# Rounded weight parts by casting transfers instead of ScalarE in group two's input blocks, and a lane step tied to the split one k-step earlier

## The chip, the cores and the metric

The kernel runs on one core of one Trainium2 chip. The metric is the device time of one execution in microseconds; lower is better. Three runs of the kernel before gave 1782.76, 1782.76 and 1781.36 us, median 1782.76 us.

## What is computed

One layer of a bidirectional hybrid encoder is applied to two requests (1024 and 256 tokens, model width 2048):

```python
hn = rms_norm(x, norm_g)
proj = hn @ w_in                        # 2048 -> 4896
xbc, z_ssd, dt_raw, q, k, v, z_att, mq, z_mem = split_cols(proj, IN_SIZES)
o_ssd = rms_norm(ssd(silu(conv(xbc)), dt) * silu(z_ssd))
o_att = window_attention(rms_norm(q), rms_norm(k), v, sink) * silu(z_att)
mk, mv = split_cols(rms_norm(mem) @ w_mem_kv, ...)
o_mem = softmax(rms_norm(mq) @ rms_norm(mk).T) @ mv * silu(z_mem)
y = x + concat[o_ssd, o_att, o_mem] @ w_out
```

All arrays are float32. The large products are done with rounded parts: a float32 value is split into h, the value rounded to the type that TensorE multiplies quickly (float32r), and l, the rounded rest, and a product is the sum of h·h, h·l and l·h.

## The kernel before

**Groups and blocks.** The 1280 tokens make two groups of five 128-token tiles each. The program goes through them in blocks. Most of group one's input columns and the last half of group two's output are multiplied in pairs (`block_pair`, from line 1257); these and the memory's blocks are not touched by the change. Group two's input blocks come in this order: x0 to x5, kv, q, za0, za1, z0, z1, mq, zm0, zm1. Of these kv, q, z0, z1 and mq are built by `block_tok`, 16 k-steps each: a k-step takes one 128-row slice of the weights (512 columns, 288 for kv) and does three matmuls for each of five token tiles. The ten x, za and zm blocks are built by `block_feat`, 8 steps each of two slices of 256 columns, with 24 matmuls of 320 columns in a step. In both the last two steps are run together, tile by tile, so that the first accumulators are finished early. These 15 blocks have 160 weight loads. Then follow the four blocks o0 to o3 of the output, again by `block_tok`.

**A k-step's weights.** SyncE loads the slice into `wraw` (four buffers, `RB`). `wsplit` (line 204) makes the parts: ScalarE copies `wraw` to `wh` (line 206), VectorE subtracts `wh` from `wraw` to give `wl` (line 207). `wh` and `wl` have three buffers each (`WB`): the parts of step k can be written once the matmuls of step k-3 have run, while TensorE has the steps k-2 and k-1 in front of it.

**Lanes.** Beside the blocks runs all else: convolution, state-space scan, attention, normalisations. It is written as generators in two queues, `lanes`. After each k-step `pump` (line 158) takes some steps from them, at rates given by the table `RATES`. `step` (line 144) runs one of them:

```python
for ins in marks:
    st.enter_context(tc.issue_after(ins))
next(gen)
```

`issue_after` puts every instruction that the step issues on an engine behind `ins` on that engine's queue. `marks` holds the two instructions of the last `wsplit`: so a lane step's ScalarE work stands behind the last ScalarE split, and its VectorE work behind the last VectorE split. GpSimd does small things for the lanes: the power in a reciprocal root (lines 123 and 124), copies and clears of `lg`, `lgw` and `mprw` (lines 683 and 635); no mark names an instruction of GpSimd.

**Order on the engines.** Each engine runs its instructions in the order in which they stand. A scheduler sets that order from its own estimate of when operands are there; the splits are traced with a priority that is 100 places higher (`HP[2]`).

Of the kernel before, what the change touches and what calls it, by code (L numbers as in the profile page):

```python
# [10 lines left out]
F32 = mybir.dt.float32  # L11
# [10 lines left out]
KT = D // P  # L22
# [9 lines left out]
RATES = ({'kv': (4.0, 1.0), 'z1': (2.2, 1.7)},  # L32
         {'kv': (1.5, 1.5), 'x': (2.1, 2.15), 'q': (2.25, 2.5), 'za': (2.15, 2.5), 'z0': (2.1, 2.5),
          'z1': (2.1, 2.55), 'mq': (2.0, 2.7), 'zm': (1.75, 2.75), 'o': (2.15, 2.4)})
# [10 lines left out]
def hymba_encoder_kernel(  # L45
# [7 lines left out]
    V, A, G, T, S = nc.vector, nc.scalar, nc.gpsimd, nc.tensor, nc.sync  # L53
# [48 lines left out]
    def dram(shape, name):  # L102
        return dr.tile(shape, F32, tag=name, name=name)
# [5 lines left out]
    q_d = [dram([P, 512], f"q_{t}") for t in range(NT)]  # L109
# [28 lines left out]
    def queue(lane, fn, ts):  # L138
        for t in ts:
            lanes[lane].append(((fn.__name__, t), fn(t)))  # L140

    marks = []

    def step(lane):
        name, gen = lane[0]
# [32 lines left out]
    pend, loaded = deque(), deque()  # L178
# [25 lines left out]
    def wsplit(raw, h, l):  # L204

        a = A.activation(h, raw, AF.Copy)  # L206
        b = V.tensor_sub(l, raw, h.bitcast(F32))  # L207
        marks[:] = a.ins, b.ins

    def w_laid(src, n):  # L210

        def load(k, raw):
            S.dma_start(raw, src[k])
        return load, n

    def laid_in(name):
        o, n, tok_ = W_AT[name]
        flat = w_in_laid[o:o + D * n]
        return flat.rearrange("(k p c) -> k p c", p=P, c=n if tok_ else 512)

    def w_in_rows(name):
        return w_laid(laid_in(name), W_AT[name][1])
# [8 lines left out]
    TURNED = [4 * q + m for q in (0, 2, 1, 3) for m in range(4)]  # L231
    PAIRED = [k + 8 * i for k in range(8) for i in range(2)]

    def block_tok(w, nt, evac, before_last=None, feats=range(KT), places=range(KT)):

        load, n = w
        ps = [acc.tile([P, 512], F32, tag="acc", name="acc") for _ in range(nt)]
        hls = {}
        for k in range(KT):
            raw = wp.tile([P, 512], F32, tag="wraw", name="wraw", bufs=RB)  # L240
            load(feats[k], raw[:, :n])
            with tc.high_priority(offset=HP[2]):
                h = wp.tile([P, 512], F32R, tag="wh", name="wh", bufs=WB)
                l = wp.tile([P, 512], F32R, tag="wl", name="wl", bufs=WB)
                wsplit(raw[:, :n], h[:, :n], l[:, :n])
            hls[k] = h, l
            if k == KT - 2:
                continue
            if k == KT - 1 and before_last is not None:
                before_last(k)  # L250

            for t in range(nt):
                for k_ in ((k - 1, k) if k == KT - 1 else (k,)):
                    q, m = divmod(places[k_], 4)
                    h, l = hls[k_]
                    sh = cur["H", q][:, m, t * P:(t + 1) * P]
                    sl = cur["L", q][:, m, t * P:(t + 1) * P]
                    T.matmul(ps[t][:, :n], sh, h[:, :n], start=(k_ == 0), stop=False)  # L258
                    T.matmul(ps[t][:, :n], sh, l[:, :n], start=False, stop=False)  # L259
                    T.matmul(ps[t][:, :n], sl, h[:, :n], start=False, stop=(k_ == KT - 1))  # L260
                if k == KT - 1:
                    with tc.high_priority(offset=HP[0]):
                        evac(t, ps[t])
            if k == KT - 1:
                yield k - 1
            yield k

    def block_feat(name, evac):

        ps = [[acc.tile([P, 512], F32, tag="acc", name="acc") for _ in range(2)] for _ in range(2)]  # L270
        src = laid_in(name)
        hls = {}
        for kk in range(KT // 2):
            raw = wp.tile([P, 512], F32, tag="wraw", name="wraw", bufs=RB)
            S.dma_start(raw, src[kk])
            with tc.high_priority(offset=HP[2]):
                h = wp.tile([P, 2, 256], F32R, tag="wh", name="wh", bufs=WB)
                l = wp.tile([P, 2, 256], F32R, tag="wl", name="wl", bufs=WB)
                wsplit(raw, h.rearrange("p a c -> p (a c)"), l.rearrange("p a c -> p (a c)"))
            hls[kk] = h, l  # L280
            if kk == KT // 2 - 2:
                continue
            tail = kk == KT // 2 - 1

            for kks in ([(kk - 1, kk)] if tail else [(kk,)]):
                for f in range(2):
                    for k in [2 * x + j for x in kks for j in range(2)]:
                        q, m = divmod(k, 4)
                        sh, sl = [x[:, k % 2, f * P:(f + 1) * P] for x in hls[k // 2]]
                        for half in range(2):  # L290
                            c = slice(half * 320, half * 320 + 320)
                            o = ps[f][half][:, :320]
                            T.matmul(o, sh, cur["H", q][:, m, c], start=(k == 0), stop=False)  # L293
                            T.matmul(o, sh, cur["L", q][:, m, c], start=False, stop=False)  # L294
                            T.matmul(o, sl, cur["H", q][:, m, c], start=False, stop=(k == KT - 1))  # L295
                    if tail and f == 0:
                        with tc.high_priority(offset=HP[1]):
                            evac(0, ps[0])
            for k in range(2 * kks[0], 2 * kk + 2):
                yield k  # L300
        with tc.high_priority(offset=HP[1]):
            evac(1, ps[1])
# [20 lines left out]
    def ev_raw(dst, base):  # L323
        def f(i, ps):
            z = ev.tile([P, 512], F32, tag="evt" if i % 2 else "evu", name="qs")
            A.activation(z, ps, AF.Copy)
            S.dma_start(dst[base + i], z)
        return f

    def ev_dtkv(base):  # L330
        def f(i, ps):
            t = base + i
            r = ev.tile([P, P], F32, tag="evt" if i % 2 else "evu", name="kraw")
            A.activation(r, ps[:, 32:160], AF.Copy)
            S.dma_start(k_d[t], r)
            V.tensor_add(dt_all[:, t, :], ps[:, :32], dtb)
            V.tensor_copy(v_all[:, i + (2 if base else 0), :], ps[:, 160:288])  # L337
        return f


    left = deque()

    def some_left():
        with ExitStack() as st:
            for ins in marks:
                st.enter_context(tc.issue_after(ins))
            left.popleft()()
# [800 lines left out]
    raw, sums, rows = {}, {}, {}  # L1148
# [301 lines left out]
    def run(gen, rates, after=None, hold=0, lag=2, extra=None):  # L1450

        for k in gen:
            if after is not None:
                pend.extend(after(k))
            if hold:
                for _ in range(2 if k < KT - 4 else 0):
                    if pend:
                        u = pend.popleft()()
                        next(u)
                        next(u)  # L1460
            else:

                if loaded and (len(loaded) == lag or not pend or k >= KT - 4):
                    next(loaded.popleft())
                if pend and k < KT - 4:
                    loaded.append(pend.popleft()())
                    next(loaded[-1])

            if k >= hold:
                pump(rates)  # L1470
            if extra is not None:
                extra(k)
# [99 lines left out]
    run(block_tok(w_mem_rows(1), 4, ev_mv, places=TURNED), MR[1], extra=p_step)  # L1572

    def tok(name, w, evac, after=None, grp=0):
        run(block_tok(w, 5, evac), RATES[grp][name], after)

    def feat(name, b, evac, grp, after=None, extra=None):
        run(block_feat(f"{name}{b}", evac), [r / 2 for r in RATES[grp][name]], after, lag=3, extra=extra)
# [2 lines left out]
        extra=lambda k: p_step(16 + k))  # L1581
# [5 lines left out]
    for u, unit in enumerate(units):  # L1587
# [42 lines left out]
    w_kv = w_in_rows("kv")  # L1630
    run(block_tok(w_kv, 5, ev_dtkv(0), before_last=lambda _: need(vectors, [0])), RATES[0]["kv"], hold=5,
        extra=lambda k: some_left() if left else None)
# [4 lines left out]
    def when_done(n, then):  # L1637

        told = []

        def f(k):
            for _ in range(n):
                if left:
                    some_left()
            if not left and not told:
                told.append(then())
        return f
# [3 lines left out]
        extra=when_done(1, lambda: queue(1, ssd_up, range(4))))  # L1651
# [10 lines left out]

    need(attn, range(4))
    kv_shift()
    run(block_tok(w_kv, 5, ev_dtkv(5)), RATES[1]["kv"], extra=lambda k: some_left() if left else None)
    queue(0, k_prep, range(5, 10))
    queue(0, attn, [4])
    queue(1, dt_prep, [5])
    run(block_tok(w_in_rows("q"), 5, ev_raw(q_d, 5)), RATES[1]["q"], extra=when_done(2, lambda: queue(1, ssd_up, range(4, 8))))
    gate("za", 0)  # L1670
    queue(0, attn, range(5, 10))
    tok("z0", w_in_rows("z0"), ev_gate(0, 5), grp=1)
# [106 lines left out]
```

## Time and profile before

| | us |
|---|---|
| median of three runs | 1782.76 |
| the profiled execution, its own time | 1782.24 |
| its span, first to last instruction | 1780.5 |
| TensorE (PE) busy in the span | 1766.1 |
| VectorE (DVE) busy | 1245.5 |
| ScalarE (ACT) busy | 918.6 |
| GpSimd (POOL) busy | 550.2 |

In the rows of the profile a line such as `L207 DVE ... wl<-wraw,wh` names the code line, the engine, what is written and what is read; "idle before" is the time for which that engine stood still just before, with what ended it. A row of the windows view gives a stretch of the execution (us from the start) and each engine's busy time in it. The two lines of `wsplit` are one helper for all callers, so their groups mix all blocks unless a window or a tile is named. Group two's input blocks run from 589.6 us (x0) to 1318.6 us (end of zm1).

### The profile page before, as it was taken

To read this page: it belongs to the slowest core of one execution; us is meant where nothing else is said; L and a number is where in the kernel's file an instruction comes from. 1 tells how busy PE (TensorE), PEld (TensorE's weight loads), DVE (VectorE), ACT (ScalarE), POOL (GpSimd) and SP (SyncE) were. 2 spreads that over 40 slices of the span, in tenths; PEclk is the share of its full clock that TensorE was granted. 3 is DMA by queue.
4 is the path that set the end of the run, shared out by engine and by line. 5 is a ranking of instruction groups with operands and counts; after the bars stand their busy time and mean duration, and the time that the engine had idled before them with its cause. 6 is when DMAs were issued, how large, how long until landed. Compare 5 with 4: busy or idle time off the path is not lost.

```text
span 1780.5 us, 31950 instructions
## 1 busy us (share of the span) xinstructions
PE 1766.1 (99%) x11046; PEld 1611.0 (90%) x11046; DVE 1245.5 (70%) x2348; ACT 918.6 (52%) x2049; POOL 550.2 (31%) x960
## 2 busy tenths in 40 slices
PE   9999999999999999999999999999999999999999
PEld 7889999999998999999889988887988888889999
DVE  5596788888868877877765676557777654766665
ACT  5555455554434766656464566544446633543332
POOL 0105899998810110011000100011100000058775
PEclk9999999999999999999999999999999999999999
DMA  8553454445446644453635655557777854644442
GB/s 302 192 182 124 136 153 148 142 142 164 123 145 202 196 131 135 149 166 101 193 121 179 197 151 161 170 161 248 223 239 230 255 188 141 221 145 143 148 142 78
DMA packets 208211, 301.16 MB, mean 169 GB/s; under 512 B 19569, under 2 KB 86193, under 8 KB 208049
## 3 DMA queue, kind: packets, MB, share of 16 engines
q1 hardware_dynamic: 207904, 299.06, 53.6%
q8 instruction: 87, 1.43, 0.3%
q14 instruction: 76, 0.61, 0.1%
q10 hardware_dynamic: 144, 0.06, 0.0%
HBM read 236.36 MB, written 62.69 MB: 168 GB/s over the span
## 4 chain that ended last, share of the span: by engine, by line
PE 88%; DVE 5%; issue 3%; DMA 2%; ACT 1%; POOL 1%; SPq 0%; POOLq 0%; DVEq 0%; ACTq 0%
PE acc L258 11%; PE acc L260 10%; PE acc L259 10%; PE acc L1288 7%; PE acc L1286 7%; PE acc L1287 7%; PE acc L293 5%; PE acc L295 5%; PE acc L294 5%; PE accm L1287 3%; PE accm L1286 3%; PE accm L1288 3%; PE po L723 1%; PE py L988 1%; DVE wl L207 1%
## 5 line engine op out<-in xcount | busy, mean ns | idle before, releaser
L207 DVE TENSOR_TENSOR wl<-wraw,wh 128x512 fp32r<-128x512 f32 (+1 forms) x480 | 347.4, 725 | 229.9 <-ACT wh L206 224.3
L206 ACT ACTIVATE wh<-wraw 128x512 fp32r<-128x512 f32 (+1 forms) x480 | 292.1, 613 | 297.1 <-PE acc L260 150.5
L258 PE MATMUL acc<-wh,xH 128*128 128x512 f32 (+1 forms) x1088 | 418.7, 385 | 0.2 <-DVE v_all L337 0.2
L260 PE MATMUL acc<-wh,xL 128*128 128x512 f32 (+1 forms) x1088 | 410.1, 377 | 0.0
L259 PE MATMUL acc<-wl,xH 128*128 128x512 f32 (+1 forms) x1088 | 409.7, 377 | 0.0
L258 PEld LDWEIGHTS acc<-wh,xH 128*128 128x128 f32 x1088 | 204.5, 188 | 36.9 <-issue 2.9
L260 PEld LDWEIGHTS acc<-wh,xL 128*128 128x128 f32 x1088 | 204.2, 188 | 37.0 <-issue 0.2
L259 PEld LDWEIGHTS acc<-wl,xH 128*128 128x128 f32 x1088 | 204.6, 188 | 35.3 <-issue 1.2
L293 PE MATMUL acc<-xH,wh 128*128 128x320 f32 x640 | 202.5, 316 | 0.2 <-DVE zs L309 0.2
L294 PE MATMUL acc<-xL,wh 128*128 128x320 f32 x640 | 198.9, 311 | 0.0
L295 PE MATMUL acc<-xH,wl 128*128 128x320 f32 x640 | 198.2, 310 | 0.0
L206 ACT ACTIVATE sh<-ws 128x384 fp32r<-128x384 f32 x176 | 91.2, 523 | 207.1 <-POOL ws L1254 103.4
L207 DVE TENSOR_TENSOR sl<-ws,sh 128x384 fp32r<-128x384 f32 x176 | 124.2, 709 | 95.8 <-ACT sh L206 94.0
L1254 POOL TENSOR_TENSOR ws<-wraw 128x128 f32<-128x128 f32 x176 | 111.1, 631 | 208.8 <-DMA wraw<-in_w_in_pairs_dram 93.6
L293 PEld LDWEIGHTS acc<-xH,wh 128*128 128x128 f32 x640 | 120.1, 188 | 2.7 <-issue 1.9
L294 PEld LDWEIGHTS acc<-xL,wh 128*128 128x128 f32 x640 | 120.2, 188 | 1.7 <-issue 1.4
L1254 POOL TENSOR_TENSOR ws<-wraw,ws 128x128 f32<-128x128 f32 x176 | 117.5, 667 | 13.8
L295 PEld LDWEIGHTS acc<-xH,wl 128*128 128x128 f32 x640 | 120.2, 188 | 0.7 <-issue 0.6
L1254 POOL TENSOR_TENSOR wraw<-wraw 128x128 f32<-128x128 f32 x176 | 112.6, 640 | 13.7
L1254 POOL TENSOR_TENSOR ws<-ws,wraw 128x128 f32<-128x128 f32 x176 | 116.2, 660 | 0.0
L635 POOL MEMSET lgw<- 128x1 f32 x40 | 3.9, 98 | 315.9 <-DVE lg L698 227.0
L362 DVE SCALAR_TENSOR_TENSOR c<-u,vec,c 128x638 f32<-128x638 f32 (+1 forms) x96 | 90.0, 939 | 9.1 <-ACT c L357 8.7
(439 smaller groups left out, 3951.0 us busy)
## 6 DMA issues: line engine op xcount, KB each, us to landing
wraw<-in_w_in_laid_dram SPq DMA_DIRECT2D x176, 256.0 KB, 2.9
wraw<-in_w_in_pairs_dram SPq DMA_DIRECT2D x112, 256.0 KB, 2.7
wraw<-in_w_out_laid_dram SPq DMA_DIRECT2D x64, 256.0 KB, 3.5
wraw<-in_w_out_pairs_dram SPq DMA_DIRECT2D x64, 256.0 KB, 2.7
rf<-ac SPq DMA_DIRECT2D x40, 256.0 KB, 4.1
rb<-ac SPq DMA_DIRECT2D x40, 256.0 KB, 4.8
wraw<-in_w_mem_laid_dram SPq DMA_DIRECT2D x32, 256.0 KB, 4.4
xst<-in_x_sample_dram SPq DMA_DIRECT2D x20, 256.0 KB, 5.7
```

The costliest lines, as they stand in the source:

```text
L206: a = A.activation(h, raw, AF.Copy)
L207: b = V.tensor_sub(l, raw, h.bitcast(F32))
L258: T.matmul(ps[t][:, :n], sh, h[:, :n], start=(k_ == 0), stop=False)
L259: T.matmul(ps[t][:, :n], sh, l[:, :n], start=False, stop=False)
L260: T.matmul(ps[t][:, :n], sl, h[:, :n], start=False, stop=(k_ == KT - 1))
L293: T.matmul(o, sh, cur["H", q][:, m, c], start=(k == 0), stop=False)
L294: T.matmul(o, sh, cur["L", q][:, m, c], start=False, stop=False)
L295: T.matmul(o, sl, cur["H", q][:, m, c], start=False, stop=(k == KT - 1))
L1254: G.tensor_tensor(out=o, in0=x, in1=y, op=op)
L1286: T.matmul(ps[p], h, xh, start=(k_ == 0), stop=False)
L1287: T.matmul(ps[p], h, xl, start=False, stop=False)
L1288: T.matmul(ps[p], l, xh, start=False, stop=(k_ == 7))
```

## The change

In the 15 input blocks of group two the ScalarE copy goes. In its place GpSimd issues a second transfer of the same weight slice from DRAM straight into `wh`; as the types differ (float32 and float32r), this transfer rounds on its way. `wraw` is still loaded by SyncE, and VectorE still subtracts `wh` from it. The marks also change there: a lane step is no longer tied to this step's splits but to the VectorE split of the k-step before, and it has no mark on ScalarE at all. The blocks q, kv and z1 of group one, the four o blocks, the memory's blocks and the pair blocks keep `wsplit`.

```diff
-    marks = []
+    marks, latest = [], []
...
         a = A.activation(h, raw, AF.Copy)
         b = V.tensor_sub(l, raw, h.bitcast(F32))
         marks[:] = a.ins, b.ins
+        latest[:] = [b.ins]
+
+    def wsplit_loaded(raw, h, l, src):
+
+        G.dma_start(h, src)
+        b = V.tensor_sub(l, raw, h.bitcast(F32))
+        marks[:] = latest
+        latest[:] = [b.ins]
...
-            load(feats[k], raw[:, :n])
+            S.dma_start(raw[:, :n], src[feats[k]])
...
-                wsplit(raw[:, :n], h[:, :n], l[:, :n])
+                if loaded:
+                    wsplit_loaded(raw[:, :n], h[:, :n], l[:, :n], src[feats[k]])
+                else:
+                    wsplit(raw[:, :n], h[:, :n], l[:, :n])
...
-                wsplit(raw, h.rearrange("p a c -> p (a c)"), l.rearrange("p a c -> p (a c)"))
+                wsplit_loaded(raw, h.rearrange("p a c -> p (a c)"), l.rearrange("p a c -> p (a c)"), src[kk])
...
-        run(block_tok(w, 5, evac), RATES[grp][name], after)
+        run(block_tok(w, 5, evac, loaded=name != "o"), RATES[grp][name], after)
...
-    run(block_tok(w_kv, 5, ev_dtkv(5)), RATES[1]["kv"], extra=lambda k: some_left() if left else None)
+    run(block_tok(w_kv, 5, ev_dtkv(5), loaded=True), RATES[1]["kv"], extra=lambda k: some_left() if left else None)
...
-    run(block_tok(w_in_rows("q"), 5, ev_raw(q_d, 5)), RATES[1]["q"], extra=when_done(2, lambda: queue(1, ssd_up, range(4, 8))))
+    run(block_tok(w_in_rows("q"), 5, ev_raw(q_d, 5), loaded=True), RATES[1]["q"], extra=when_done(2, lambda: queue(1, ssd_up, range(4, 8))))
```

Nine lines are added above, so a line of the code after is up to nine higher than the same line before. The next rows are GpSimd's queue at the end of group one's block z1 and the start of x0, before. `krr` is the reciprocal root in the normalisation of the keys (`k_prep`), `qr` that of the queries.

```order
L123 TENSOR_SCALAR krr<-kss 128x2
L124 TENSOR_TENSOR krr<-krr,mhalf 128x2
L123 TENSOR_SCALAR krr<-kss 128x2
L124 TENSOR_TENSOR krr<-krr,mhalf 128x2
L683 COPY lg<-nsink 128x2
```

The same place after:

```order
L213 DMA wh<-in_w_in_laid_dram 128x512
L123 TENSOR_SCALAR krr<-kss 128x2
L124 TENSOR_TENSOR krr<-krr,mhalf 128x2
L213 DMA wh<-in_w_in_laid_dram 128x512 x4
L123 TENSOR_SCALAR krr<-kss 128x2
L124 TENSOR_TENSOR krr<-krr,mhalf 128x2
L692 COPY lg<-nsink 128x2
L213 DMA wh<-in_w_in_laid_dram 128x512 x3
```

The first of these casting transfers, of x0's step 0, stands ahead of one pair of `krr`; those of steps 1 to 4 stand behind it, those of steps 5 to 7 behind the next pair and a copy. On SyncE's queue the load of the keys for the first of these pairs stood behind the load of `wraw` for x0's step 4, and now stands ahead of it. The next rows are VectorE's queue at the same place, before: `zs` takes z1's accumulators out of PSUM, `kss` is the sum that `krr` is made from, `kr` the keys that it scales.

```order
L309 SCALAR_TENSOR_TENSOR zs<-zs,acc 128x512 x2
L518 TENSOR_REDUCE kss<-ksq 128x2
L207 TENSOR_TENSOR wl<-wraw,wh 128x512
L950 COPY state<-pst 128x512
L309 SCALAR_TENSOR_TENSOR zs<-zs,acc 128x512
L207 TENSOR_TENSOR wl<-wraw,wh 128x512
L539 CAST kT<-pk 128x2x128
L523 TENSOR_TENSOR kr<-kr,krr 128x128
```

And after:

```order
L214 TENSOR_TENSOR wl<-wraw,wh 128x512
L318 SCALAR_TENSOR_TENSOR zs<-zs,acc 128x512 x2
L527 TENSOR_REDUCE kss<-ksq 128x2
L318 SCALAR_TENSOR_TENSOR zs<-zs,acc 128x512
L532 TENSOR_TENSOR kr<-kr,krr 128x128
L194 SCALAR_TENSOR_TENSOR chd<-chd,vec,rbc 128x640
L318 SCALAR_TENSOR_TENSOR zs<-zs,acc 128x512
L533 TENSOR_TENSOR kr<-kr,gq 128x128
L198 TENSOR_TENSOR xL_7441<-chd,xH_7440 128x640
L318 SCALAR_TENSOR_TENSOR zs<-zs,acc 128x512
L959 COPY state<-pst 128x512
L214 TENSOR_TENSOR wl<-wraw,wh 128x512 x2
```

The splits of steps 1 and 2 moved behind lane work that stood behind them, and two of the five `zs` now stand behind a `kr` that waits for GpSimd. The last place is GpSimd's queue in the block kv; `mr` is the reciprocal root for the memory's queries. Before:

```order
L123 TENSOR_SCALAR mr<-mss 128x4
L124 TENSOR_TENSOR mr<-mr,mhalf 128x4
L635 MEMSET mprw 128x1 x2
L123 TENSOR_SCALAR mr<-mss 128x4
L124 TENSOR_TENSOR mr<-mr,mhalf 128x4
L635 MEMSET mprw 128x1 x2
```

After:

```order
L123 TENSOR_SCALAR mr<-mss 128x4
L124 TENSOR_TENSOR mr<-mr,mhalf 128x4
L213 DMA wh<-in_w_in_laid_dram 128x288 x2
L644 MEMSET mprw 128x1 x2
L213 DMA wh<-in_w_in_laid_dram 128x288 x5
L123 TENSOR_SCALAR mr<-mss 128x4
L124 TENSOR_TENSOR mr<-mr,mhalf 128x4
L213 DMA wh<-in_w_in_laid_dram 128x288 x3
L644 MEMSET mprw 128x1
L213 DMA wh<-in_w_in_laid_dram 128x288 x2
```

Here the transfers of kv's steps 10, 11 and 12 stand behind the second `mr` pair.

## The prediction on record

> **What bounds the kernel now.** I read the page's first part first, then the windows of group two's input blocks, then who waits for whom in them.
>
> ```profile
> span 1780.5 us, 31950 instructions
> PE 1766.1 (99%) x11046; PEld 1611.0 (90%) x11046; DVE 1245.5 (70%) x2348; ACT 918.6 (52%) x2049; POOL 550.2 (31%) x960
> ```
>
> TensorE (PE) is idle for 14.4 us of 1780.5. Its order and its work do not change in amount, so the time can only move by what TensorE waits, before and after. The part that the change touches, x0 to zm1, and two blocks of it (kv, then z0 with z1), in columns length, PE, PEld, DVE, ACT, POOL:
>
> ```profile
> 589.60:1318.60 729.00, 723.68 (x4851) 649.75 (x4849) 509.77 (x1125) 417.87 (x1046) 68.60 (x165) 1.00 0.54 169
> 818.40:865.20 46.80, 45.50 (x363) 43.85 (x362) 36.99 (x84) 33.04 (x89) 6.47 (x9) 1.00 0.56 162
> 1006.30:1159.70 153.40, 153.40 (x928) 127.09 (x927) 92.36 (x203) 89.60 (x221) 10.70 (x33) 1.00 0.56 174
> ```
>
> In these 729 us TensorE is idle for 5.3 us. No change here can gain more than about that. ScalarE (ACT) is busy 57% and VectorE (DVE) 70%: neither bounds the stretch. What TensorE waits for in it:
>
> ```profile
> PE psc L689 <- ACT qT L673: 2.4, 1, 2.4
> PE pmt L628 <- DVE mpr L805: 1.3, 1, 1.3
> PE psc L689 <- DVE nm L691: 0.7, 1, 0.7
> PE psc L689 <- DVE xs L909: 0.3, 1, 0.3
> PE acc L293 <- DVE zs L309: 0.2, 1, 0.2
> ```
>
> These five sum to 4.9 us, in matmuls of the lanes but for the last one; none is a wait for a weight part. So today the splits are always in time, and the ScalarE copy that goes is not on the path.
>
> **What the change removes.** ScalarE's copies in this stretch (line 206), and the waits that they held in the queues of ScalarE and VectorE:
>
> ```profile
> 589.60:1318.60 729.00, 98.62 (x162) 1.00 0.54 169
> DVE wl L207 <- ACT wh L206: 92.4, 57, 5.1
> ACT wh L206 <- PE acc L260: 57.9, 29, 5.3
> ACT wh L206 <- PE acc L294: 30.0, 21, 4.2
> ```
>
> Of 417.87 us of ScalarE's work 98.62 go, with two rows of waits for free buffers of 87.9 us in which lane work stood behind a copy. All of it lies beside TensorE's 723.68 us. VectorE stood 92.4 us before a split for ScalarE, and still TensorE waited 4.9 us: the lanes have room. What can come back is therefore a part of the 4.9 us. Bounds: 0 and -4.9. I take -1.0, since the largest wait (2.4 us, on ScalarE's qT) is one that a freer ScalarE may shorten, while the scheduler has also moved the lane matmuls themselves.
>
> **What it adds.** 160 casting transfers on GpSimd's queue. The trace of before has no transfer issued by GpSimd, so its time from issue to landing is bounded by other rows: the same slices from SyncE, the slowest common 256 KB load of this stretch, and the mean of a GpSimd instruction.
>
> ```profile
> wraw<-in_w_in_laid_dram SPq DMA_DIRECT2D x139, 256.0 KB, 2.9
> rb<-ac SPq DMA_DIRECT2D x28, 256.0 KB, 4.8
> wraw<-in_w_in_laid_dram SPq DMA_DIRECT2D x16, 144.0 KB, 2.5
> L1254 POOL TENSOR_TENSOR ws<-wraw,ws 128x128 f32<-128x128 f32 x176 | 117.5, 667 | 13.8
> L207 DVE TENSOR_TENSOR wl<-wraw,wh 128x512 fp32r<-128x512 f32 (+1 forms) x480 | 347.4, 725 | 229.9 <-ACT wh L206 224.3
> ```
>
> Lower bound 2.9 us, upper 4.8 + 0.67 = 5.5 us. I take 2.9 + 0.67 = 3.6 us, nearest to the row with the same bytes and source, plus one GpSimd instruction for issuing it. With the subtraction, 0.725 us, the path from "may be issued" to "parts ready" is 4.3 us (3.6 to 6.2). For kv, 2.5 + 0.67 and a subtraction of 0.45 us (row below): 3.6 us. Today the path is a copy and a subtraction. The Trainium skill (DMA: Bandwidth & Descriptors, Anatomy of one DMA) fits a transfer issued by GpSimd with 2.0 us plus bytes over 436 GB/s, 2.6 us for 256 KB as an estimate; with that the path is 3.3 us, and the first term below falls by 1.0 us.
>
> *Is the path hidden?* With three buffers it has two k-steps of TensorE. From the windows: kv 2 x 46.80/16 = 5.85 us, z0 and z1 2 x 153.40/32 = 9.6 us. At a block's edge the last two steps are run together and free two buffers at their end, so step 1 of the next block has about one step, 153.40/32 = 4.8 us. At 4.3 us all of these cover the transfer, the edges barely; at 6.2 us kv and the edges do not.
>
> *The queue is what uncovers it.* GpSimd works in order, and its lane instructions, which waited for VectorE at no cost, now stand ahead of transfers. First place, x0's step 1, whose transfer stands behind a `krr` pair:
>
> ```profile
> 587.67 0.39 PE L260 MATMUL acc<-wh,xL 128*128 128x512 f32 x1
> 592.40 0.56 POOL L123 TENSOR_SCALAR krr<-kss 128x2 f32<-128x2 f32 x1 [7.71 <-DVE kss L518]
> 593.04 0.70 POOL L124 TENSOR_TENSOR krr<-krr,mhalf 128x2 f32<-128x2 f32 x1
> 593.59 0.31 PE L293 MATMUL acc<-xH,wh 128*128 128x320 f32 x1
> ```
>
> The buffer is free at 588.1 (its last reader, 587.67 + 0.39), the first matmul of step 1 runs at 593.59. Behind the `krr` pair the transfer starts at 593.74, and the parts are there at 593.74 + 4.3 = 598.0: 4.4 us late (3.7 to 6.3 with the bounds of the path). Against that, the load of these keys no longer stands behind a weight load on SyncE's queue, so `krr` can come some 1 to 2.5 us sooner: 1.2 us at the least. I take 4.4 - 1.4 = +3.0 us. The `zs` that stand behind `kr` on VectorE wait for the same `krr` and hold x0's accumulators, inside the same 3 us. The transfers of steps 2 to 4 follow one issue apart, with TensorE already late; they cost nothing more.
>
> Second place, kv's step 10, whose transfer stands behind an `mr` pair:
>
> ```profile
> 841.39 0.29 PE L260 MATMUL acc<-wh,xL 128*128 128x288 f32 x1
> 842.45 0.57 POOL L123 TENSOR_SCALAR mr<-mss 128x4 f32<-128x4 f32 x1 [13.75 <-DVE mss L769]
> 843.10 3.12 POOL L124 TENSOR_TENSOR mr<-mr,mhalf 128x4 f32<-128x4 f32 x1
> 843.68 0.45 DVE L207 TENSOR_TENSOR wl<-wraw,wh 128x288 fp32r<-128x288 f32 x1
> 846.92 0.29 PE L258 MATMUL acc<-wh,xH 128*128 128x288 f32 x1
> ```
>
> The pair ends at 846.22; 846.22 + 3.6 = 849.8 against 846.92 gives 2.9 us late. If line 124 takes 0.70 us here, as in the row at 593.04, the pair ends at 843.8 and the parts are ready at 847.4: 0.5 us late. I take +2.0 us, nearer to the row at the place itself. If kv's transfers take the upper bound, kv alone adds about 5.
>
> *What stands behind the transfers.* GpSimd's lane work gets at most one issue, 0.67 us, in front of each piece: 160 x 0.67 = 107 us on top of 68.60 in 729, a quarter of the time; taken at nothing, hidden by the lanes' room shown above, and at most some 2 us if it is not. On VectorE a split now waits for a landing, but the marks let lane work go ahead of it: nothing, up to the loss of rival three. SyncE's load of step k+4 waits for the later split of step k; four steps of kv are 11.7 us against a load of 2.5 us: nothing. The extra 40 MB in 729 us are 55 GB/s on 169; in proportion the engines' share rises from 0.54 to 0.72: nothing.
>
> Sum: +3.0 (x0) + 2.0 (kv) - 1.0 (lane waits) = **+4.0 us** on the execution's own 1782.24 (span 1780.5 and 1.7 around it). The median of the runs is 0.5 us higher; on it the forecast is **1786.8 us**. A measurement of this kernel can tell about 0.2%, 3.6 us, from no change; the forecast is just beyond that.
>
> **The rivals.**
>
> One, not slower: the transfers are covered and the lane waits go. It decides at the `krr` pair: if it ends by 589.3 (593.59 - 4.3), 4.4 us sooner than now, x0 loses nothing, and likewise kv when `mr` ends by 843.3. Then what remains is 0 to -4.9 us: 1777.9 to 1782.8. For it: VectorE and ScalarE are freer, and both pairs wait for VectorE. Against it: in the new order of VectorE `kss` stands behind x0's first split, which itself waits for a transfer.
>
> Two, slow transfers: GpSimd cannot write a transfer's descriptors while VectorE runs certain operations, and the path grows to about 7 us. Then kv's two steps (5.85 us) and some 14 block edges (4.8 us) are short: 16 x (6.7 + 2.9 - 3 x 2.9)/3 = 5 us in kv, the edges 14 x about 1 us, x0 6 us: with the rest +20 to +30, 1803 to 1813. The Trainium skill (SBUF — State Buffer, SBUF: two separate sides) describes this lock for VectorE's two-port operations, with a 620 ns transfer becoming 3100 ns; no row here shows a transfer of GpSimd. Against it: VectorE's costly groups here (line 207) are two-input subtractions, which that page does not count among them; so a small chance.
>
> Three, the lanes come late: each split waits on VectorE for its landing and holds lane work, TensorE then waits for the lanes as it does in the five rows above, +5 to +10 us: 1788 to 1793. Against it: 92.4 us of such waits cost 4.9 us today.
>
> **How the numbers follow.** Forecast case 0.50 (0.38 slower, 0.12 within), rival one 0.30 (0.15 faster, 0.15 within), rival two 0.10, rival three 0.10 (0.07 slower, 0.03 within): faster 0.15, within 0.30, slower 0.55. The range goes from 1778.0, near rival one's best, to 1800.0: the forecast with its upper bounds is 6.3 + 5 and some 6 at the edges, +17, without the gain. Rival two and the tails are left out.
>
> **What would show it.** Right: ScalarE's busy time in group two falls by some 98 us with TensorE's unchanged; at x0's step 1 TensorE waits about 3 us for a VectorE split that itself waited for a transfer, with a `krr` ending just before the issue; at kv's step 10 about 2 us; hardly any such wait in z0 to zm1. Wrong: no wait of TensorE on a weight part over 1 us (rival one); waits at most block edges and along kv (rival two); longer waits at lines 689 and 628 (rival three); or transfers that land in under 2.5 or over 5.5 us.

## The result and the profile after

The changed kernel takes 1873.53 us (median of four runs, 1865.4 to 1874.28) against 1782.76 us before: a ratio of 1.050, interval [1.048, 1.052]. The forecast was 1786.8 us, at most 1800. It is slower, as said, but by 91 us where 4 were foreseen.

The profiled execution (1874.28 us) shows where. First the head of the page, then the windows view over group two's input blocks, x0 to zm1 (columns as in the prediction: stretch, length, PE, PEld, DVE, ACT, POOL, clock, share of the DMA engines, GB/s):

```profile
span 1872.5 us, 31981 instructions
PE 1801.4 (96%) x11046; PEld 1627.9 (87%) x11046; DVE 1246.2 (67%) x2348; ACT 839.7 (45%) x1889; POOL 631.9 (34%) x1120
```

```profile
593.20:1412.40 819.20, 757.03 (x4848) 665.42 (x4849) 511.59 (x1125) 334.92 (x874) 149.54 (x324) 0.98 0.67 199
```

These blocks took 729.0 us before and take 819.2 now: 90.2 us of the 92.0 by which the span grew. ScalarE has 83 us less to do (98 were foreseen) and VectorE as much as before; neither bounds the stretch. TensorE was idle for 5.3 us and now is for 62.2; its busy time rose by 33 us with the same matmuls. A VectorE half of a split is the subtraction that makes `wl`. The next rows are these halves with what they waited for, and GpSimd's casting transfers:

```profile
L214 DVE TENSOR_TENSOR wl<-wraw,wh 128x512 fp32r<-128x512 f32 (+1 forms) x159 | 105.6, 666 | 196.2 <-DMA wh<-in_w_in_laid_dram 100.5 <-issue 51.1 <-PE acc L269 14.9
L213 POOL DMA_DIRECT2D wh<-in_w_in_laid_dram x160 | 87.5, 547 | 405.0 <-PE acc L304 118.1 <-PE acc L269 94.2 <-PE acc L303 76.4
wh<-in_w_in_laid_dram POOLq DMA_DIRECT2D x143, 256.0 KB, 3.7
wh<-in_w_in_laid_dram POOLq DMA_DIRECT2D x16, 144.0 KB, 3.2
```

VectorE stands idle for 196.2 us ahead of 159 halves. The row names the landing for 100.5 of them and puts 51.1 under "issue", where the profile shows no releaser. The landing times in the trace settle it: every half that VectorE stood idle for, 94 of 160, starts within 0.2 us of the landing of its own cast. Before it was this, nearly all of it for ScalarE's copy:

```profile
L207 DVE TENSOR_TENSOR wl<-wraw,wh 128x512 fp32r<-128x512 f32 (+1 forms) x162 | 107.7, 665 | 93.3 <-ACT wh L206 92.4
```

In the median the transfers land as fast as foreseen (3.7 us against an estimate of 3.6; kv's 3.2); 18 of the 160 take more than 5.5 us, the longest 6.95. It is what TensorE waits for that is not as foreseen: most of it is for the lanes, some 50 us in all rows of this view, against 10 for weight parts. The longest rows:

```profile
PE psc L698 <- DVE nm L700: 5.4, 4, 2.1
PE psc L698 <- ACT qT L682: 4.9, 3, 2.4
PE ppt L637 <- DVE lg L707: 4.8, 4, 2.9
PE acc L267 <- DMA wh<-in_w_in_laid_dram: 4.5, 4, 2.1
PE pk L545 <- DVE xs L918: 3.9, 1, 3.9
PE ppt L637 <- DVE nm L700: 3.8, 4, 1.4
```

One place shows how the two hang together, from za0's last step into za1. The timeline of GpSimd, of VectorE, and of TensorE (start, length, engine and line, in brackets the idle time ahead and what ended it):

```profile
997.52 0.53 POOL L213 DMA_DIRECT2D wh<-in_w_in_laid_dram  x1 [5.08 <-PE acc L304]
1001.04 0.53 POOL L213 DMA_DIRECT2D wh<-in_w_in_laid_dram  x1 [2.99 <-PE acc L303]
1008.87 0.19 POOL L123 TENSOR_SCALAR krr<-kss 128x2 f32<-128x2 f32 x1 [7.30 <-DVE kss L527]
1009.15 1.12 POOL L124 TENSOR_TENSOR krr<-krr,mhalf 128x2 f32<-128x2 f32 x1
1010.24 1.14 POOL L213 DMA_DIRECT2D wh<-in_w_in_laid_dram  x2
```

```profile
1003.61 0.69 DVE L214 TENSOR_TENSOR wl<-wraw,wh 128x512 fp32r<-128x512 f32 x1 [8.02 <-DMA wh<-in_w_in_laid_dram]
1004.22 0.42 DVE L548 CAST kT<-pk 128x256 fp32r<-128x256 f32 x1
...
1008.50 0.28 DVE L527 TENSOR_REDUCE kss<-ksq 128x2 f32<-128x128 f32 x1
...
1014.59 0.69 DVE L214 TENSOR_TENSOR wl<-wraw,wh 128x512 fp32r<-128x512 f32 x1 [1.24 <-issue]
1015.20 0.68 DVE L918 COPY xs<-pxs 128x512 f32<-128x512 f32 x1
```

```profile
1011.81 0.31 PE L302 MATMUL acc<-xH,wh 128*128 128x320 f32 x1
1016.03 0.56 PE L545 MATMUL pk<-identr,kh 128*128 128x128 f32 x4 [3.91 <-DVE xs L918]
1016.38 0.60 PE L303 MATMUL acc<-xL,wh 128*128 128x320 f32 x1
1016.78 0.47 PE L304 MATMUL acc<-xH,wl 128*128 128x320 f32 x1
```

GpSimd gets the buffer at 997.5 and issues. VectorE has nothing else in front, and stands for 8.02 us until that transfer has landed, 5.9 us after its issue. All lane work that is queued behind this half is late: `kss`, then `krr` on GpSimd (which stood idle for 7.30 us), then the two casts behind `krr`, then the next halves, and `xs` behind one of those, for which TensorE stops for 3.91 us. So a late cast makes lane work late, which makes TensorE and the next casts late.

The windows view right after shows a second loss. The matmuls at 1016.4 follow each other at half the clock:

```profile
1012.00:1016.00 4.00, 0.12 (x1) 0.00 (x1) 2.73 (x7) 1.58 (x5) 0.00 (x0) 1.00 0.90 311
1016.40:1019.80 3.40, 3.40 (x15) 3.40 (x14) 3.40 (x8) 0.38 (x1) 0.00 (x0) 0.51 0.53 148
1019.90:1025.00 5.10, 5.10 (x31) 4.49 (x31) 2.75 (x7) 2.81 (x7) 1.44 (x3) 1.00 0.58 156
```

Of such stretches the trace has 11 in group two, 41 us together, and before none; at half the speed that is some 20 us of the 33 by which TensorE's busy time grew. The other 13 were not traced to a cause. The Trainium skill (TensorE: Matmul & The Clock Gate, Part 1: The HAM clock gate) has the clock halved after an idle window of 3413 ns. The length agrees with the trace; how idle the stretch before was is taken up in the last section.

### The profile page after: what moved, and what is told of

Read it like the earlier page. It is cut to its first block, busy times and chain, and to the rows that moved or that the text cites. A ratio compares the mean times of both kernels' runs of the same rounds, so it can differ in the third digit from the quotient of the medians.

```text
span 1872.5 us, 31981 instructions
## 1 busy us (share of the span) xinstructions
PE 1801.4 (96%) x11046; PEld 1627.9 (87%) x11046; DVE 1246.2 (67%) x2348; ACT 839.7 (45%) x1889; POOL 631.9 (34%) x1120
## 5 line engine op out<-in xcount | busy, mean ns | idle before, releaser
L268 PE MATMUL acc<-wl,xH 128*128 128x512 f32 (+1 forms) x1088 | 414.0, 381 | 2.9 <-DVE wl L214 2.6
L206 ACT ACTIVATE wh<-wraw 128x512 fp32r<-128x512 f32 (+1 forms) x320 | 194.8, 615 | 167.1 <-PE acc L269 86.7
L214 DVE TENSOR_TENSOR wl<-wraw,wh 128x512 fp32r<-128x512 f32 (+1 forms) x160 | 106.3, 666 | 197.9 <-DMA wh<-in_w_in_laid_dram 100.5
L213 POOL DMA_DIRECT2D wh<-in_w_in_laid_dram x160 | 87.5, 547 | 405.0 <-PE acc L304 118.1
L302 PE MATMUL acc<-xH,wh 128*128 128x320 f32 x640 | 207.1, 324 | 4.3 <-DVE zs L318 2.2
L304 PE MATMUL acc<-xH,wl 128*128 128x320 f32 x640 | 202.7, 317 | 1.0 <-DVE wl L214 1.0
```

What stands on the lines that cost most here:

```text
L213: G.dma_start(h, src)
```

## The experiments

Four theories stood at the start. **One**: VectorE waits for the landing and holds the lane work queued behind (the prediction's rival three, at some ten times its price). **Two**: GpSimd's queue couples casts and lane work. **Three**: the changed marks alone. **Four**: the added transfers slow the lanes' loads. A fifth came later. Where a run has one raw buffer less, its time outside group two grows (shown by a control), so group two's blocks are compared, 729.0 us before. Each of these times is of one profiled execution. The whole times of one kernel's executions lie 2 to 18 us apart, so a difference of a few us between two runs is not sure. All diffs are against the kernel after, that of the control against the kernel before. A table of all runs follows them.

**The marks alone.**

```diff
-        G.dma_start(h, src)
+        A.activation(h, raw, AF.Copy)
```

> The changed kernel with one thing put back: in group two's input blocks ScalarE copies the raw weights to the rounded part again, and no casting transfer is made. What stays of the change is the order alone: lane steps stand behind the VectorE half of the split made one k-step sooner, and behind no ScalarE half. Theory one (the VectorE half waits for a transfer's landing, and lane work queued behind it waits with it): the landing is gone, so 1775 to 1795 us. Theory two (GpSimd's queue couples casts and lane work): the casts are gone, 1775 to 1795 us as well. Theory three (the freer order of lane work by itself lets ScalarE and VectorE stand waiting for loads that come later): most of the 91 us stay, 1840 us or more. Theory four (the added transfers slow the lanes' loads): 1775 to 1795 us.

1803.43 us, ratio 1.011 [1.009, 1.013]; group two 752.7. Theory three has a quarter of the loss when alone. Without its mark, ScalarE's lane work was ordered earlier and stands waiting for loads; these rows had 1.8 us and none before:

```profile
ACT rf L980 <- DMA rf<-ac: 44.1, 24, 3.8
ACT rb L980 <- DMA rb<-ac: 28.3, 16, 5.2
```

**Casts, tied to this step's half.** `marks[:] = [b.ins]` in place of `latest`.

> The casts stay, and each lane step stands behind the VectorE half of its own k-step's split, not of the one made a k-step sooner. Theory one: the lane work now stands behind a half whose cast was issued last, so its wait for the landing is longer still: 1873 us or later, up to 1950. Theory three (the marks are what costs): back to some 1780 to 1800 us. Theories two and four say nothing of the marks: about 1873 us, within 15.

1878.54 us, group two 825.6: 6 us later than the change there. Theory three falls as the main cause. The 6 us go with theory one, but lie within the 15 that theories two and four allow. The sooner mark on VectorE is no cost.

**A fourth buffer for rounded parts**, under the changed kernel and, as control, under the one before.

```diff
-CH, WB, RB, WA, WBB = 4, 3, 4, 5, 4
+CH, WB, RB, WA, WBB = 4, 3, 3, 5, 4
...
-                h = wp.tile([P, 512], F32R, tag="wh", name="wh", bufs=WB)
+                h = wp.tile([P, 512], F32R, tag="wh", name="wh", bufs=WB + 1)
```

> The casts and the marks stay; there are four buffers for rounded parts in place of three (one buffer for raw weights less, three for four, which pays for the space). A cast may go out one k-step sooner, about 5 us, which is more than its landing takes (median 3.7 us), while the VectorE half stands where it stood, tied to its own three buffers. All transfers stay, and so does GpSimd's work. Theory one: the cast has landed when the VectorE half's turn comes, the waits of VectorE for the landing (100.5 us) fall below 25 us, and most of the loss comes back: 1780 to 1805 us. Theory two: the casts still stand in GpSimd's queue beside lane work, but wait for a buffer that comes free sooner: half the loss back, 1810 to 1850 us. Theories three and four: little comes back, 1850 to 1880 us.

> The control for the run with four buffers for rounded parts: the kernel before, with that one change of buffers (four rounded, three raw). Rounded parts come from ScalarE here and wait for no landing of their own, so no theory expects a gain from the fourth buffer; a raw weight loaded a step later may cost a little: 1780 to 1800 us by each of the theories.

1880.56 and 1814.02 us; group two 794.7 and 730.9. Of the control's 31 us, 23 lie ahead of group two, 2 in it and some 6 behind it; later expectations put all 31 ahead. Beside its control the fourth buffer brings back 25 of the 90 us, not most of them. VectorE's idle time ahead of the halves only fell to 138.3 us. The view names the landing for 37.9 of them, but by the landing times in the trace 97 of the 138 us end within 0.3 us of the landing of the half's own cast. So the buffer hid the landing only in part, and this run does not say what theory one is worth.

**A GpSimd copy instead of the transfer.** `G.tensor_copy(h, raw)` in place of the cast; it takes 0.71 us each.

> The changed kernel with its casting transfer replaced by a copy on GpSimd from the raw weights to the rounded part, at the same place in GpSimd's queue and with the same marks. No landing and no added traffic is left; GpSimd still stands waiting for a rounded part's buffer, with lane work queued behind it. So far the marks alone cost 20 us, all 91; a fourth buffer took back about 25 of the casts' cost in group two. Theory one (VectorE held by the landing): 1800 to 1825 us. Theory two (GpSimd's queue, tied to TensorE by each cast, holds lane work): 1840 us or more. Theory four (the added traffic): 1800 to 1820 us. A copy that takes much longer on GpSimd than the 0.75 us that VectorE's half takes would spoil the test; then its duration is what is read.

1813.61 us, group two 761.8: 9 us over the marks alone. GpSimd stood 305 us for TensorE's buffers in the two largest rows, with the casts 318 in the four largest, so theory two has at most some 10 us, and the cost lies in the transfer: its landing, its traffic or its issue.

**A casting transfer beside the copy**, unused, into a spare tile.

> ScalarE's copy and the changed marks, and beside them a casting transfer per step into a spare tile that nothing reads (unused work; ScalarE writes one column of the spare tile first, so that the transfers keep the pace of the splits; one raw buffer less makes the space, which by the control costs 31 us ahead of group two and 1 us in it). Group two's blocks take 729 us before, 751 with the marks alone, 819 with the change. Traffic and GpSimd's issue are all here, and nothing that computes waits for a landing. Theory one: group two in 751 to 765 us. Theory two, since GpSimd's queue is tied to the splits here too, only later by a ScalarE copy: 770 to 810 us. Theory four: 790 us or more.

1906.64 us, group two 830.3, later than the change itself. It looked like theory four, but the edit had put a landing wait on ScalarE, which writes a column of the one spare tile:

```profile
ACT spare L216 <- DMA spare<-in_w_in_laid_dram: 154.5, 87, 4.5
```

So it does not tell traffic from landing. The same transfers without this wait (the run with the bytes alone, below) take 788.2 us, 42 less: a wait for a landing costs on ScalarE too.

**Lane work off GpSimd**, without and with the fourth buffer.

```diff
-        G.memset(w.bitcast(F32)[...
+        V.memset(w.bitcast(F32)[...
...
-            G.tensor_copy(lg[:, :, nk:nk + 1], ns8[:, rr, :].unsqueeze(2))
+            V.tensor_copy(lg[:, :, nk:nk + 1], ns8[:, rr, :].unsqueeze(2))
```

> The changed kernel, with the clears of one column and the copies of two columns of the attention slots (87 of GpSimd's 133 small lane instructions with their waits) on VectorE, where the data come from, instead of GpSimd. What is left on GpSimd beside the casts are the reciprocal roots. Theory two: GpSimd's queue is what couples, so at least a third of the loss comes back: below 1845 us. Theories one and four: no gain, or some us later by VectorE's added work (87 x some 0.1 us): 1870 to 1890 us.

> The same, with four buffers for rounded parts and three for raw weights. Group two took 795 us with four buffers alone, 819 with the change, 751 with the marks alone. If the landing on VectorE (theory one) and GpSimd's queue (theory two) are the two causes, little of either is left: group two in 750 to 770 us, the whole near 1840 (the buffer's 31 us ahead of group two among it). Theory four (traffic): group two stays at 785 us or more.

1866.06 and 1878.31 us; group two 813.1 and 788.8, 6 us better each, which is no more than executions of one kernel differ by. Theory two, which wanted less than 1845 us, falls as a main cause.

**The landing without the bytes.** ScalarE copies 496 columns, a cast brings 16.

```diff
-        G.dma_start(h, src)
+        G.dma_start(h[:, :16], src[:, :16])
+        A.activation(h[:, 16:], raw[:, 16:], AF.Copy)
```

> ScalarE's copy and the changed marks; of each rounded part only the first 16 of 512 columns (8 KB of 256 KB) come by a casting transfer, the others by ScalarE. VectorE's half and TensorE still wait for a landing, with next to no added traffic. So far: marks alone 752 us in group two, 1803 in all; the change 819 and 1873; a GpSimd copy without landing or traffic 762 and 1814. Theory one (the wait for the landing): most of the 57 us between 762 and 819 is here, group two 790 us or more. Theory four (the traffic): 752 to 770 us.

1838.26 us, group two 784.0: 31 over the marks alone, in between what the two theories gave. The landing costs, though these land in 2.7 us.

**The bytes without the landing**, by GpSimd and by SyncE, into a spare tile.

```diff
+        A.activation(h, raw, AF.Copy)
+        spare = wp.tile([P, 512], F32R, tag="spare", name="spare", bufs=1)[:, :src.shape[-1]]
+        go = sm.tile([P, 1], F32, tag="go", name="go", bufs=2)
+        g = G.tensor_copy(go, h[:, :1].bitcast(F32))
+        with tc.issue_after(g.ins):
+            G.dma_start(spare, src)
```

> ScalarE's copy and the changed marks, and beside them a casting transfer per step into a spare tile that nothing reads (unused work). This time it is GpSimd alone that waits for the pace (a copy of one column of the rounded part) and for the spare tile, no computing engine waits for a landing. One raw buffer less makes the space, worth 31 us ahead of group two and 1 in it, so group two is what counts: marks alone 752 us, the change 819. Theory four (traffic): 785 us or more. Theory one: 752 to 768 us.

> The same bytes a second time, but as plain loads from SyncE's queue into the spare tile (unused work), each right behind the raw weight's load; GpSimd issues nothing. If it is the bytes (HBM and the 16 DMA engines) that cost, group two as in the run with the casting transfers beside, within 15 us. If it is GpSimd's queue and what it does to VectorE or to the landing, group two is back at 752 to 768 us. SyncE may stand waiting for the spare tile with lane loads behind it; that would show as its waits and add to the time.

1869.29 and 1845.6 us; group two 788.2 and 765.0. The same bytes cost 35 us from GpSimd's queue and 12 from SyncE's. GpSimd here stood 170.4 us for the spare tile's last landing, with lane work queued behind.

**ScalarE's mark back.** `a = A.activation(h, raw, AF.Copy)` and `marks[:] = [a.ins] + latest`.

> ScalarE's copy; lane work on ScalarE stands behind the copy of its own k-step, as before the change, and on VectorE behind the half made a k-step sooner, as changed. It splits the 20 us that the changed marks cost. If ScalarE's missing mark is the cause (with it gone, ScalarE stands waiting for lane loads, 74 us in group two): back to 1778 to 1790 us. If VectorE's sooner mark is: 1797 to 1810 us.

1780.24 us, ratio 0.9993 [0.998, 1.000]: as before the change, group two 728.6. The 20 us of the marks were ScalarE's missing mark. Without casts, the sooner mark on VectorE brings and costs nothing.

Theory **five**, then: landing and traffic cost only since ScalarE has lost its mark. Four runs put it back.

> The run with casting transfers into a spare tile (unused work, GpSimd alone waits for its pace), with ScalarE's mark back: lane work on ScalarE stands behind the copy of its own k-step. Group two so far: before 729 us, ScalarE's mark back and nothing else of the casts 729, marks alone 753, traffic beside the changed marks 788. If the costs simply add, group two takes 729 + 35 = 764 us. Theory five (without its mark ScalarE stands waiting for lane loads, and every load that traffic makes later is paid there; with the mark the loads have time to spare): 745 us or less.

> The run in which 16 of the 512 columns come by a cast, with ScalarE's mark back. If the costs add: group two 729 + 31 = 760 us. Theory five: VectorE still waits for the landing (79.8 us in group two without the mark), but the lanes have time to spare again: 745 us or less.

```diff
-        G.dma_start(h, src)
+        a = A.activation(h[:, :16], raw[:, :16], AF.Copy)
+        G.dma_start(h[:, 16:], src[:, 16:])
...
-        marks[:] = latest
+        marks[:] = [a.ins] + latest
```

> The change with an anchor: ScalarE makes the first 16 columns of each rounded part (some 0.2 us each), the cast the other 496, and lane work on ScalarE stands behind this small copy of its own k-step. Landing and traffic are both here in full. If the costs add: group two 729 + 31 + 35 = 795 us, 1840 in all. Theory five: 729 to 755 us, 1780 to 1808 in all.

> The same with four buffers for rounded parts and three for raw weights (31 us ahead of group two). The landing is mostly hidden. If the costs add: group two about 729 + 35 + 6 = 770 us. Theory five: 729 to 745 us.

1855.88, 1820.63, 1863.8 and 1866.95 us; group two 778.4, 767.7, 815.2 and 781.1, where theory five wanted at most 745 (755 for the third). It falls: with the real casts the mark is worth 4 us of 90 in group two (10 by the medians of the whole). The windows view of the third, and VectorE's halves in the landing run, the third and the fourth:

```profile
592.30:1407.50 815.20, 755.34 (x4851) 665.95 (x4851) 511.42 (x1124) 357.23 (x1040) 150.81 (x322) 0.97 0.67 198
```

```profile
L215 DVE TENSOR_TENSOR wl<-wraw,wh 128x512 fp32r<-128x512 f32 (+1 forms) x159 | 105.5, 665 | 142.6 <-DMA wh<-in_w_in_laid_dram 62.6 <-issue 25.9 <-DMA rb<-ac 12.3
```

```profile
L215 DVE TENSOR_TENSOR wl<-wraw,wh 128x512 fp32r<-128x512 f32 (+1 forms) x159 | 105.6, 665 | 195.2 <-DMA wh<-in_w_in_laid_dram 111.6 <-issue 48.9 <-PE py L998 5.3
```

```profile
L215 DVE TENSOR_TENSOR wl<-wraw,wh 128x512 fp32r<-128x512 f32 (+1 forms) x159 | 105.6, 664 | 142.1 <-DMA wh<-in_w_in_laid_dram 46.1 <-PE acc L269 29.8 <-PE acc L305 18.3
```

Over these runs and the one with the mark and no casts, group two's time goes with the idle time in the third column: 76.2 us and 728.6 with the mark and no cast, 142.6 and 767.7 with small casts, 195.2 and 815.2 with whole ones, and with a fourth buffer back to 142.1 and 781.1. Here too 101 of the 142.1 us end within 0.3 us of a cast's landing. The idle time by itself does not set the time: the control with four buffers has 106.8 us of it and takes 730.9.

**What in the transfers costs?** The traffic run with ScalarE's mark once more, cut to 16 columns; and SyncE's loads with the mark.

```diff
-            G.dma_start(spare, src)
+            G.dma_start(spare[:, :16], src[:, :16])
```

> The run with ScalarE's mark and casting transfers into a spare tile (778 us in group two, 50 over the 728.6 of the same marks alone), with each spare transfer cut to 16 of its 512 columns (unused work). GpSimd waits at the same places and issues as many transfers; the bytes are gone. If the bytes cost (theory four): group two 729 to 740 us. If what costs is that GpSimd's queue is tied to the splits and issues a transfer per step (theory two): 760 us or more.

> ScalarE's mark, and the bytes a second time as plain loads from SyncE's queue (unused work; SyncE itself waited 100 us for the spare tile in the run without the mark). If the bytes cost: 765 us or more in group two. If GpSimd's part in them costs: 729 to 745 us.

1819.86 and 1815.77 us; group two 738.2 and 736.8. By what was expected, the first says that the bytes cost, and the second that GpSimd's part in them does; so neither alone is the 50 us. GpSimd's queue and issue alone cost 10 us over the 728.6 of the same marks, the bytes alone 8; up to 2 of each is the raw buffer less, by the control. These sizes are rough: beside the control's 1814.02 us, which also has three raw buffers, the medians of the whole are 6 and 2 us later. The windows of the two:

```profile
616.60:1354.80 738.20, 726.13 (x4851) 651.33 (x4850) 511.67 (x1124) 416.90 (x1044) 219.84 (x483) 1.00 0.58 168
```

```profile
615.90:1352.70 736.80, 725.73 (x4851) 649.87 (x4850) 510.21 (x1124) 415.50 (x1045) 66.19 (x165) 1.00 0.70 220
```

The second has the DMA engines busier (0.70) than the change itself (0.67), and TensorE idle for 11 us in all. So the 50 us of the traffic run by GpSimd are not the bytes as such. What the trace shows in it are GpSimd's waits for the spare tile's landing, with lane work queued behind; in the short transfers' run they are half as long. That these waits are the 50 us is argued, not shown:

```profile
POOL spare L219 <- DMA spare<-in_w_in_laid_dram: 218.0, 93, 6.1
```

```profile
POOL spare L219 <- DMA spare<-in_w_in_laid_dram: 102.8, 49, 4.9
```

| run | median us | group two us | VectorE idle ahead of its halves |
|---|---|---|---|
| before | 1782.76 | 729.0 | 93.3 |
| after | 1873.53 | 819.2 | 196.2 |
| ScalarE's mark back, no casts | 1780.24 | 728.6 | 76.2 |
| marks alone | 1803.43 | 752.7 | 93.8 |
| GpSimd copy | 1813.61 | 761.8 | 92.7 |
| bytes by SyncE, without / with the mark | 1845.6 / 1815.77 | 765.0 / 736.8 | 90.7 / 68.0 |
| GpSimd issue of 8 KB, with the mark | 1819.86 | 738.2 | 81.6 |
| bytes by GpSimd, without / with the mark | 1869.29 / 1855.88 | 788.2 / 778.4 | 106.0 / 90.8 |
| landing of 8 KB, without / with the mark | 1838.26 / 1820.63 | 784.0 / 767.7 | 157.9 / 142.6 |
| casts, four buffers, without / with the mark | 1880.56 / 1866.95 | 794.7 / 781.1 | 138.3 / 142.1 |
| casts with the mark | 1863.8 | 815.2 | 195.2 |
| casts, tied to this step's half | 1878.54 | 825.6 | 202.9 |
| control: before, with four buffers | 1814.02 | 730.9 | 106.8 |
| casts, lane work off GpSimd, three / four buffers | 1866.06 / 1878.31 | 813.1 / 788.8 | 184.2 / 129.8 |
| bytes by GpSimd, with ScalarE's wait for the spare tile | 1906.64 | 830.3 | 111.1 |

**What is shown and what stays open.** The marks cost 24 us alone and 4 to 10 beside the casts; the bytes 8 and GpSimd's issue 10, each beside ScalarE's mark and each at most that. A VectorE half that waits for a landing costs 39 us with small transfers, some 30 of them beyond the run in which GpSimd issues the same small transfers and no half waits for them (738.2). With whole transfers it is 87, bytes included; starting the casts a step sooner takes 34 of those back. Of the 52 us left with four buffers, bytes and issue account for at most 18 by themselves. The other 34 are only argued: VectorE is still idle for 142 us there, 101 of them up to a landing, the rest largely for TensorE itself. That the full-size transfers of GpSimd have a further cost of their own, beside GpSimd's wait for the spare tile, was not separated. No version beat the kernel before.

## Why the prediction was wrong, point by point

- **The room of TensorE, "No change here can gain more than about that"**: right, and the term of -1.0 us did not come: TensorE's idle time rose from 5.3 to 62.2 us, and ScalarE's 83 us bought nothing that shows.
- **The path of a cast**: right in the median. Landing 3.7 and 3.2 us against 3.6 and, for kv, 3.2 with the issue. The upper bound of 5.5 us was too low for 18 of 160.
- **x0, +3.0 us**: the place, the cause and nearly the size were right, the size in part by luck. The `krr` pair runs at 594.03, the casts go at 594.99, VectorE's two halves run at 599.74; TensorE waits 1.39 us for the cast and 1 us for a `zs`. Counted from the start of x0, `krr` came 2.3 us sooner where 1.4 was taken, and the cast took 4.7 us where 3.6 was taken. x0 takes 36.3 us against 31.4, so +4.9; 1.7 of these are the clock at half, from 599.9:

```profile
594.99 1.15 POOL L213 DMA_DIRECT2D wh<-in_w_in_laid_dram  x2
```

```profile
599.74 1.31 DVE L214 TENSOR_TENSOR wl<-wraw,wh 128x512 fp32r<-128x512 f32 x2 [0.87 <-DMA wh<-in_w_in_laid_dram]
```

```profile
599.76 0.52 PE L302 MATMUL acc<-xH,wh 128*128 128x320 f32 x1 [1.39 <-DMA wh<-in_w_in_laid_dram]
```

- **kv, +2.0 us**: at step 10 the `mr` pair ends at 872.45 and TensorE waits 2.14 us for the cast behind it, as foreseen; but kv as a whole takes 54.4 us against 46.8. Other halves wait as well, one of them 3.80 us. The rows are of GpSimd at step 10, of VectorE at that other half, and of TensorE at step 10:

```profile
872.45 1.14 POOL L213 DMA_DIRECT2D wh<-in_w_in_laid_dram  x2
```

```profile
862.07 0.46 DVE L214 TENSOR_TENSOR wl<-wraw,wh 128x288 fp32r<-128x288 f32 x1 [3.80 <-DMA wh<-in_w_in_laid_dram]
```

```profile
876.97 0.40 PE L267 MATMUL acc<-wh,xH 128*128 128x288 f32 x1 [2.14 <-DMA wh<-in_w_in_laid_dram]
```

- **"hardly any such wait in z0 to zm1"**: right for the weight parts, for which TensorE waits 1.8 us in z0 and z1. Yet x0 and kv, the two places foreseen, lose only 12.5 of the 90 us, and z0 and z1 lose 26: 179.5 us against 153.4, with TensorE idle for 14.0 us, nearly all of it for lane work, and its clock at 0.95:

```profile
1051.00:1230.50 179.50, 165.51 (x926) 132.01 (x927) 94.92 (x207) 71.21 (x184) 26.77 (x65) 0.95 0.64 190
```

- **"On VectorE a split now waits for a landing, but the marks let lane work go ahead of it: nothing, up to the loss of rival three"**: this step failed, and with it rival three's price of 5 to 10 us. The mark lets the order place lane work ahead of a half, but what had been placed behind it waits all the same, as `kss` did behind the half of 1003.61. The argument that "92.4 us of such waits cost 4.9 us today" took waits that had no cost as room for twice as many. Those waits follow TensorE: once a buffer is free, the copy takes 0.6 us (98.62 us for 162), and the half can run. A cast takes 3.7 us in the median from its issue, and the half and all behind it stand that much longer: 39 us lost with small casts and 87 with whole ones, in the runs above.
- **GpSimd's lane work "at most some 2 us"**: up to 10 us with its issue and its pace; 6 back, hardly clear of the spread, when two thirds of the small work moved away.
- **The bytes, "nothing"**: up to 8 us. The share of the DMA engines came out at 0.67 against the 0.72 foreseen.
- **ScalarE without a mark** had no term. Alone it costs 24 us, in the change 4 to 10.
- **Rival two, a path of 7 us**: did not happen; the transfers took 3.7 us in the median. The lock that the Trainium skill describes (SBUF — State Buffer, SBUF: two separate sides) does not show in these rows: an issue takes GpSimd 0.547 us. What made 18 casts take over 5.5 us was not tested; SyncE's transfers under way beside them took 5.1 us in the mean, beside casts of under 4 us 3.1.
- **The clock** had no term: 41 us at half of it.

## What to carry to other kernels

Idle time of an engine off the critical path is no measure of room: ask what it follows, and what stands behind the waiting instruction. Here a wait for a landing, in the queue of an in-order engine that also serves the bound engine, was paid by all that was queued behind it, and came back through the buffers. A buffer ahead took back only 25 to 34 us of it; the short copy had cost nothing. When an instruction that anchored the order on its engine goes, put another anchor there: here that was worth 24 us where the copies stayed.

## What the runs showed of the hardware

TensorE's clock falls to half for 3.4 us at a time, also after a stop that is shorter than that. In the windows of the changed kernel from 692.1, a stretch with 1.02 of 3.40 us busy was enough, and one busy stretch at half speed brought the clock back:

```profile
692.10:695.50 3.40, 1.02 (x7) 0.84 (x6) 3.13 (x7) 1.86 (x3) 0.00 (x0) 1.00 0.78 218
695.50:698.90 3.40, 3.40 (x15) 3.40 (x14) 1.16 (x5) 1.85 (x6) 0.00 (x0) 0.50 0.88 268
698.90:702.30 3.40, 3.40 (x24) 3.40 (x23) 3.04 (x11) 0.87 (x4) 0.63 (x2) 1.00 0.08 13
```

So the stop of 2.4 us in the first of these windows cost another 1.7. Its length alone does not decide: before the change TensorE stood 2.4 us for `qT` once (first row of its waits in the prediction), and the clock stayed at 1.00.

A casting transfer of 8 KB from GpSimd's queue took 2.6 to 2.9 us to land (median), one of 256 KB 3.7: most of the time does not depend on the size. The Trainium skill (DMA: Bandwidth & Descriptors, Anatomy of one DMA) would have 2.0 and 2.6 us, as estimates from its fit; both came out later, in stretches in which 160 to 200 GB/s were moved in all.
